# Value sums of the sample attention: two requests in the two column halves of the array, in clumps

## The chip, the cores and the metric

The kernel runs on one core of one Trainium2 chip. The metric is the device time of one execution in microseconds (us), as the median of several executions. The engines are named as in the profile: PE (TensorE, the matmul array), PEld (its weight loads), DVE (VectorE), ACT (ScalarE), POOL (GpSimd), and SP (the engine that issues nearly all transfers).

## The reference

One inference step of a decoder with two layers, for one prompt of 1024 tokens and eight sample requests of eight new tokens each, which share the weights. Each layer is a token mixer and then a SwiGLU channel mixer. The even layer's mixer is a causal convolution next to a stick-breaking attention with 8 heads of 64. For the sample requests, keys and values of 1024 past tokens lie in pages of 128 tokens; a table names the eight pages of each request. Cut to what the change touches:

```python
def stick_breaking_attention(q, k, v, bias, q_pos, k_pos):
    z = einsum('nqhd,nkhd->nhqk', q, k) * scale + bias
    mask = k_pos[None, :] < q_pos[:, None]
    log_1m = where(mask, log_sigmoid(-z), 0.0)
    after = cumsum(log_1m, axis=3, reverse=True) - log_1m
    wgt = exp(where(mask, log_sigmoid(z) + after, -inf))
    return einsum('nhqk,nkhd->nqhd', wgt, v)     # the value sums
...
gather = lambda cache, i: cache[i][page_table].reshape(8, 1024, 8, 64)
k_all = concatenate([gather(cache_k, i), k_new], axis=1)
v_all = concatenate([gather(cache_v, i), v_new], axis=1)
```

## The kernel before, in words

All tokens lie in two groups of columns: GA (the first 512 prompt tokens) and GB (the other 512 and the 64 sample tokens). A matmul of activations and weights is three array passes over split operands (`mm3`, L235). Work is in a foreground, the projections and channel mixers of a group, and a background, a chain of Python generators of which one piece is emitted at each slot of the foreground (`bg`, called as `slot` in `block`, `pair`, `out_block` and others). The order of the instructions on each engine is the order in which the Python code emits them; each engine works through its own in that order, and the framework adds the waits. While the foreground is the output projection and the channel mixer of GA, the background is `flow_c`: the prompt attention of GB, then `sample()` side by side with the convolution of GB (`conv_b`), then its normalization (`conv_norm`).

`sample()` works on four pairs of requests, `bp` 0 to 3; `b2` is the request within a pair. A score has 64 rows for a request (8 heads x 8 tokens), so a pair fills 128 rows. A unit is (pair, block of key pages, request); a unit has two steps `s`, 48 in all, 12 for a pair:

- `trans` turns three (or two) K pages by matmuls with the identity (L1112), ACT and DVE split them (`kth`, L1115 and L1116), `score` multiplies them with the queries (L1135), and `score_b` makes the sigmoids `bet` and `qf` of both requests of a pair.
- After the last unit of a pair, `weights` and `weights_b` make the stick-breaking weights by scans on DVE in three later steps, and `turned` turns them, keys onto partitions, into `wts` (L1184 on PE, L1185 on ACT): nine tiles of 128 keys x 128 columns, of which 64 belong to each request; the ninth is for the new keys.
- `pv(i)` multiplies one V page (128 keys x 512, all heads) with the 64 columns of its request (L1205), and sums in the PSUM tile `o` of 64 partitions. The pages go request after request: eight pages of `b2` 0, the new keys (`vnew`, L1211), then the copy out (`ob`, L1213), then the same for `b2` 1. Each `pv` is an item of `pvq`, and one item is taken at each of two places of a step. The tile `vst` holds two pages of one request, in two buffers; `load_v` issues two page loads on SP for it as soon as a buffer's two pages have been used.
- `o` holds every head's queries against every head's values. `fin`, one piece later, keeps the blocks where they agree: four matmuls of `ob` with columns of the constant `sel` (L1219), which turn the sums at the same time, and two ACT copies into `qall` (L1223). `sel` is made at the start of the kernel by two DVE copies of the identity.

From step 48 on there are no units left; a step then takes its items and gives way once.

## Time and profile before

| what | value |
|---|---|
| median of 3 executions | 2611.68 us (2611.19 to 2613.68) |
| span of the profiled execution | 2615.5 us |
| PE busy | 2524.0 us, 97% of the span |
| DVE, POOL, ACT busy | 65%, 60%, 42% |
| value matmuls from first to last | 675.9 to 968.5 us |
| moved over the span | 258.30 MB, 99 GB/s |

The profiled execution's own time is its span, 3.8 us above the median. A row of a group of instructions gives the line of the code, the engine, what is written from what, the count, the busy time and the mean duration in ns, and then the idle time of the engine just before these instructions with what ended it. Rows in order of time give start and length in us; consecutive alike instructions are one row. PE's durations overlap, since a matmul starts before the one ahead of it has drained; what one costs is read from start to start. "128*64" after the names is the part of the array in use, rows by columns, then come the shapes.

### The profile page before, as it was taken

The page shows a single profiled execution, that of the slowest core. Times are in us where ns is not written, and L with a number is a line of the kernel's source. Part 1 is how long each engine was busy: PE and PEld are TensorE (multiplying, and loading weights), DVE is VectorE, ACT ScalarE, POOL GpSimd, SP SyncE. Part 2 cuts the span into 40 slices and gives each one's busy share as a digit, 9 for nine tenths or more (in the row PEclk, how much of TensorE's full clock was granted, in tenths as well). Part 3 has the DMA queues.
Part 4 walks back from the last instruction along what each step waited for, and adds up shares of the span by engine and source line. Part 5 has one row for each costly group of instructions (what it writes and reads, how often), then busy time and mean ns, then how long its engine had stood idle before and what let it go on. Part 6 is the DMA issues. An engine that isn't in the chain of part 4 may idle for free.

```text
span 2615.5 us, 41225 instructions
## 1 busy us (share of the span) xinstructions
PE 2524.0 (97%) x15759; PEld 2223.2 (85%) x15759; DVE 1703.0 (65%) x2361; ACT 1109.9 (42%) x1885; POOL 1562.4 (60%) x1204
## 2 busy tenths in 40 slices
PE   8999999999999999999999999999999999999998
PEld 6788877887666657999999989989888888999997
DVE  4696777868767636276666643447777778667665
ACT  5536766744433324334433421233433334443333
POOL 6754244443333327578877732256888886987775
PEclk9999999999999999999999999999999999999999
DMA  7332241234455433422322321152233333333332
GB/s 216 113 110 72 63 115 37 73 104 128 140 145 151 131 106 100 130 73 81 91 88 83 113 78 41 45 144 63 88 96 97 93 93 92 98 92 111 89 89 77
DMA packets 355484, 258.30 MB, mean 99 GB/s; under 512 B 22913, under 2 KB 303617, under 8 KB 355272
## 3 DMA queue, kind: packets, MB, share of 16 engines
q1 hardware_dynamic: 355256, 255.66, 33.1%
q8 instruction: 125, 2.05, 0.3%
q14 instruction: 71, 0.58, 0.1%
q10 hardware_dynamic: 32, 0.01, 0.0%
HBM read 237.41 MB, written 18.69 MB: 98 GB/s over the span
## 4 chain that ended last, share of the span: by engine, by line
PE 41%; DVE 10%; POOL 2%; issue 1%; ACT 1%; POOLq 0%; DVEq 0%; ACTq 0%
PE acc L235 21%; PE acc L521 19%; DVE sum L200 2%; POOL hl L197 1%; DVE hid L241 1%; DVE hb L295 1%; DVE sum L201 1%; DVE sum L202 0%; DVE tmp L525 0%; DVE sum_c L214 0%; DVE b L1662 0%; POOL tmp L500 0%; DVE x L1662 0%; DVE fb L1666 0%; DVE xs L1666 0%
## 5 line engine op out<-in xcount | busy, mean ns | idle before, releaser
L186 POOL TENSOR_TENSOR hl<-stage,hl 128x512 fp32r<-128x512 f32 x464 | 636.4, 1395 | 507.8 <-ACT hl L184 382.4
L235 PE MATMUL acc<-x,hl 128*128 128x512 f32 (+1 forms) x3648 | 783.7, 351 | 12.2 <-DVE tmp L291 3.0
L235 PEld LDWEIGHTS acc<-x,hl 128*128 128x128 f32 x3648 | 580.3, 189 | 96.3 <-issue 30.4
L235 PE MATMUL acc<-hid,hl 128*128 128x288 f32 (+1 forms) x3096 | 555.9, 335 | 16.4 <-DVE hb L295 6.7
L235 PEld LDWEIGHTS acc<-hid,hl 128*128 128x128 f32 x3096 | 470.1, 190 | 84.1 <-issue 15.1
L295 DVE TENSOR_TENSOR hb<-acc,hb 128x512 f32<-128x512 f32 (+1 forms) x360 | 257.0, 719 | 194.8 <-PE acc L235 193.5
L521 PE MATMUL acc<-x,hl 128*128 128x288 f32 (+1 forms) x2676 | 362.1, 290 | 4.7 <-POOL hl L197 2.3
L521 PEld LDWEIGHTS acc<-x,hl 128*128 128x128 f32 x2676 | 348.9, 188 | 7.0 <-POOL hl L197 3.1
L197 POOL TENSOR_TENSOR hl<-sum,hl 128x512 fp32r<-128x512 f32 x180 | 237.1, 1345 | 176.1 <-ACT hl L196 176.1
L184 ACT ACTIVATE hl<-stage 128x1024 fp32r<-128x1024 f32 x232 | 243.5, 1054 | 229.6 <-PE acc L235 138.1
L525 DVE TENSOR_TENSOR tmp<-acc,tmp 128x288 f32<-128x288 f32 (+1 forms) x420 | 173.7, 442 | 230.7 <-ACT tmp L537 135.9
L197 POOL TENSOR_TENSOR hl<-stage,hl 128x512 fp32r<-128x512 f32 x180 | 267.7, 1509 | 13.3 <-ACT hl L196 13.3
L521 PE MATMUL acc<-b,hl 128*128 128x256 f32 (+1 forms) x1548 | 216.6, 291 | 14.8 <-DVE tmp L525 12.1
L521 PEld LDWEIGHTS acc<-b,hl 128*128 128x128 f32 x1548 | 202.2, 189 | 20.3 <-ACT hl L196 13.8
L235 PE MATMUL acc<-x1t,hl 128*128 128x288 f32 x1152 | 217.1, 296 | 1.5 <-POOL hl L186 1.5
L235 PEld LDWEIGHTS acc<-x1t,hl 128*128 128x128 f32 x1152 | 197.0, 189 | 19.7 <-POOL hl L186 1.7
L196 ACT ACTIVATE hl<-sum 128x512 fp32r<-128x512 f32 x180 | 103.1, 623 | 241.9 <-DVE sum L202 221.8
L291 DVE TENSOR_TENSOR tmp<-acc,rr 128x512 f32<-128x512 f32 (+1 forms) x108 | 75.1, 709 | 119.6 <-PE acc L235 109.5
L196 ACT ACTIVATE hl<-stage 128x512 fp32r<-128x512 f32 x180 | 105.6, 618 | 68.0 <-PE acc L235 62.7
L500 POOL TENSOR_TENSOR tmp<-tmp 128x576 f32<-128x576 f32 (+1 forms) x85 | 125.2, 1473 | 9.3 <-ACT tmp L477 8.3
L235 PE MATMUL acc<-x1a,hl 128*128 128x512 f32 x480 | 122.4, 408 | 3.0 <-POOL hl L186 1.3
L241 DVE TENSOR_TENSOR hid<-tmp,hid 128x512 fp32r<-128x512 f32 (+1 forms) x88 | 100.6, 1145 | 36.6 <-ACT hid L240 36.5
(288 smaller groups left out, 3298.1 us busy)
## 6 DMA issues: line engine op xcount, KB each, us to landing
stage<-in_w_ffn_in_dram SPq DMA_DIRECT2D x176, 512.0 KB
stage<-in_w_ffn_out_dram SPq DMA_DIRECT2D x88, 512.0 KB
stage<-in_w_in_even_dram SPq DMA_DIRECT2D x40, 512.0 KB
kst<-in_cache_k_dram SPq DMA_DIRECT2D x64, 256.0 KB
vst<-in_cache_v_dram SPq DMA_DIRECT2D x64, 256.0 KB
stage<-in_w_out_even_dram SPq DMA_DIRECT2D x16, 512.0 KB
stage<-in_w_in_odd_dram SPq DMA_DIRECT2D x16, 512.0 KB
stage<-in_w_out_odd_dram SPq DMA_DIRECT2D x16, 512.0 KB
```

Of the source, the lines that this page charges most:

```text
L184: act.activation(hl[:, 0], st, AF.Copy)
L186: pool.tensor_tensor(hl[:, 1, c], st[:, c], f32(hl[:, 0, c]), op=OP.subtract)
L196: act.activation(hl[:, 0, c], x, AF.Copy)
L197: pool.tensor_tensor(hl[:, 1, c], x, f32(hl[:, 0, c]), op=OP.subtract)
L200: todo = [lambda: dve.tensor_tensor(sb, su[:, lo], su[:, hi], op=OP.add), lambda: dve.tensor_tensor(sa[:, hi], sg[:, lo], su[:, lo], op=OP ...
L235: pe.matmul(acc[:, b, :c1 - c0], w, xs[:, xi, c0 - o:c1 - o], start=first and s == 0, stop=last and s == 2)
L241: (on or dve).tensor_tensor(dst[:, 1], src, f32(dst[:, 0]), op=OP.subtract)
L291: dve.tensor_tensor(d, a, r, op=OP.mult)
L295: dve.tensor_tensor(d, a, d, op=OP.add)
L500: (dve if both and f == NF - 1 else pool).tensor_tensor(t[:, :n], t[:, :n], u[:, :n], op=OP.mult)
L521: pe.matmul(acc[:, :w2], h[:, wi, i, k], xk[:, xi], start=k == 0 and s == 0, stop=k == 3 and s == 2)
L525: dve.tensor_tensor(out, acc[:, :w2], x, op=OP.add)
```

## The change

The two requests of a pair are summed together. `pv(i)` now takes the V page with the same number of both requests and puts their sums into the two halves of one PSUM tile `o` of 128 partitions, which are the two column halves of the array; `vst` accordingly holds one page of each. An item of `pvq` is now two such `pv` (four matmuls; with the new keys six), and during the units an item is taken only at the end of every second step. The second half of `turned`'s transposes goes through a list of its own, `soon`. The sums of both requests are copied out at once, and one selection serves both: `sel` becomes a matrix of 128 x (4 x 2 x 16) that is zero outside each request's own rows, made inside `sample()` by a memset on POOL and two ACT copies. From `pv` on there are four copies out and four selections in place of eight.

```diff
-    sel = consts.tile([128, 64], F, name="sel")
-        dve.tensor_copy(sel[0:64], ident[0:64, 0:64])
-        dve.tensor_copy(sel[64:128], ident[64:128, 64:128])
...
+            sel = sa.tile([128, 4, 2, 16], F, name="sel")
+            pool.memset(sel, 0.0)
+            for i in range(2):
+                r = slice(64 * i, 64 * i + 64)
+                act.activation(sel[r, :, i], ident[r, r].rearrange("p (h x) -> p h x", h=4), AF.Copy)
...
+                    bp, k = divmod(i, 8)
                     vst[i] = sa.tile([128, 2, 512], F, name="vst", bufs=2)
-                    for k in range(2):
-                        page_to(vst[i][:, k], cache_v, 2 * i + k)
+                    for b2 in range(2):
+                        page_to(vst[i][:, b2], cache_v, (2 * bp + b2) * 8 + k)
...
-                pvs = [lambda i=i: pv(i) for i in range(16 * bp, 16 * bp + 16)]
-                pvs[1] = lambda f=pvs[1]: (f(), new())
-                pvq.extend(first + pvs)
+                pvs = [lambda i=i: (pv(i), pv(i + 1)) for i in range(8 * bp, 8 * bp + 8, 2)]
+                pvs[0] = lambda f=pvs[0]: (f(), new())
+                soon.extend(first)
+                pvq.extend(pvs)
...
-                    osum[bp] = op_.tile([64, 512], F, name="o")
+                    osum[bp] = op_.tile([128, 512], F, name="o")
                 o = osum[bp]
-                load_v(i // 2 + 1)
-                pe.matmul(o, wts[bp][:, k, 64 * b2:64 * b2 + 64], vst[i // 2][:, k % 2], start=k == 0, stop=False)
-                if k % 2:
-                    vst.pop(i // 2)
-                    load_v(i // 2 + 3)
+                load_v(i + 1)
+                for b2 in range(2):
+                    r = slice(64 * b2, 64 * b2 + 64)
+                    pe.matmul(o[r], wts[bp][:, k, r], vst[i][:, b2], start=k == 0, stop=False)
+                vst.pop(i)
+                load_v(i + 3)
                 if k < 7:
                     return
-                pe.matmul(o, wts[bp][:, 8, 64 * b2:64 * b2 + 64], vnew, start=False, stop=True)
-                ob = tmp()[:64, 0:512]
+                for b2 in range(2):
+                    r = slice(64 * b2, 64 * b2 + 64)
+                    pe.matmul(o[r], wts[bp][:, 8, r], vnew, start=False, stop=True)
+                ob = tmp()[:, 0:512]
                 act.activation(ob, o, AF.Copy)
                 def fin():
                     for hp in range(4):
-                        pe.matmul(m[:, hp * 16:hp * 16 + 16], ob[:, hp * 128:hp * 128 + 128],
-                                  sel[:64, hp * 16:hp * 16 + 16], start=True, stop=True)
+                        pe.matmul(m[:, hp * 32:hp * 32 + 32], ob[:, hp * 128:hp * 128 + 128],
+                                  sel[:, hp].rearrange("p b x -> p (b x)"), start=True, stop=True)
...
-                if pvq:
-                    pvq.pop(0)()
+                while soon:
+                    soon.pop(0)()
                 if s < len(steps):
                     yield 2
...
-                if pvq:
+                if pvq and (s % 2 == 0 or s >= len(steps)):
                     pvq.pop(0)()
```

How the edit moves instructions on PE, first where the sums of the first pair begin (`z` are scores, `kst` K pages being turned, `acc` the foreground's matmuls, `wx` the weights of the new keys). Before, about 676 us:

```order
L1135 MATMUL z<-kth,qb 128x384 x4
L1205 MATMUL o<-vst,wts 64x512
L235 MATMUL acc<-hid,hl 128x512 x6
L1112 MATMUL m<-ident,kst 128x128 x3
L235 MATMUL acc<-hid,hl 128x512 x6
L1112 MATMUL m<-ident,kst 128x128 x3
L1205 MATMUL o<-vst,wts 64x512
L1184 MATMUL m<-ident,wx 128x128
L235 MATMUL acc<-hid,hl 128x512 x6
L1135 MATMUL z<-kth,qb 128x384 x4
L1205 MATMUL o<-vst,wts 64x512
```

The same place now, where the numbers of later lines have grown by two to eleven:

```order
L1138 MATMUL z<-kth,qb 128x384 x4
L235 MATMUL acc<-hid,hl 128x512 x6
L1115 MATMUL m<-ident,kst 128x128 x3
L235 MATMUL acc<-hid,hl 128x512 x6
L1115 MATMUL m<-ident,kst 128x128 x3
L235 MATMUL acc<-hid,hl 128x512 x6
L1138 MATMUL z<-kth,qb 128x384 x4
L1210 MATMUL o<-vst,wts 64x512 x4
L1187 MATMUL m<-ident,wx 128x128
```

Single value matmuls, two in a step, have become groups of four behind the scores of every second step. The second place is the last pair, on PE as well. Before, about 956 to 972 us:

```order
L1219 MATMUL m<-sel,tmp 128x16 x4
L1205 MATMUL o<-vst,wts 64x512 x2
L235 MATMUL acc<-x_6_77,hl 128x512 x3
L235 MATMUL acc<-x_7_78,hl 128x512 x3
L1205 MATMUL o<-vst,wts 64x512 x2
L235 MATMUL acc<-x_0_71,hl 128x512 x3
L235 MATMUL acc<-x_1_72,hl 128x512 x3
L1205 MATMUL o<-vst,wts 64x512 x2
L235 MATMUL acc<-x_2_73,hl 128x512 x3
L235 MATMUL acc<-x_3_74,hl 128x512 x3
L1205 MATMUL o<-vst,wts 64x512
L1211 MATMUL o<-vnew,wts 64x512
```

Now the whole of the last pair, from the turning of its weights to the selection:

```order
L1187 MATMUL m<-ident,bet 128x128 x8
L1210 MATMUL o<-vst,wts 64x512 x4
L1187 MATMUL m<-ident,wx 128x128
L235 MATMUL acc<-hid,hl 128x512 x6
L1210 MATMUL o<-vst,wts 64x512 x4
L235 MATMUL acc<-hid,hl 128x512 x6
L1210 MATMUL o<-vst,wts 64x512 x4
L235 MATMUL acc<-x_0_71,hl 128x512 x3
L235 MATMUL acc<-x_1_72,hl 128x512 x3
L1210 MATMUL o<-vst,wts 64x512 x4
L1217 MATMUL o<-vnew,wts 64x512 x2
```

Between two groups of four there are six matmuls of the foreground, as there were between two groups of two, and each group now reads four pages of V where one of before read two.

## The prediction, made before the changed kernel was run

> **What bounds the kernel now.** I read the page's busy time first, then the busy time by stretches around the sample attention, then the groups of the tensor engine there, and at last its order of time.

> ```profile
> span 2615.5 us, 41225 instructions
> PE 2524.0 (97%) x15759; PEld 2223.2 (85%) x15759; DVE 1703.0 (65%) x2361; ACT 1109.9 (42%) x1885; POOL 1562.4 (60%) x1204
> ```

> The tensor engine (PE) is busy for 97% of the span. Whether that holds where the edit lies is read from four stretches, one for each pair of requests whose value sums run there:

> ```profile
> core 0: us, PE busy (x) PEld busy (x) DVE busy (x) ACT busy (x) POOL busy (x), PEclk, DMA share, GB/s
> 675.90:743.20 67.30, 66.58 (x270) 41.37 (x269) 46.45 (x75) 22.25 (x46) 22.27 (x18) 1.00 0.51 146
> 768.20:834.60 66.40, 66.40 (x271) 41.49 (x270) 45.28 (x75) 23.22 (x48) 22.67 (x19) 1.00 0.50 148
> 857.40:924.60 67.20, 66.88 (x272) 41.65 (x271) 46.05 (x75) 22.06 (x45) 22.95 (x19) 1.00 0.42 126
> 934.50:971.60 37.10, 36.41 (x108) 16.54 (x108) 3.75 (x6) 6.33 (x12) 8.15 (x7) 0.92 0.43 128
> ```

> PE stands still for under 1 us in each; the next engine, DVE, is at 69% in the first three. So a microsecond taken from PE here is, to first order, a microsecond of the end. The groups that the edit touches, from 640 to 975 us:

> ```profile
> L1205 PE MATMUL o<-vst,wts 128*64 128x512 f32 x128 | 69.0, 627 | 1.9 <-ACT wts L1185 1.3 <-ACT tmp L1213 0.7
> L1219 PE MATMUL m<-sel,tmp 64*128 64x16 f32 x64 | 8.5, 262 | 0.0
> L1211 PE MATMUL o<-vnew,wts 128*64 128x512 f32 x16 | 8.2, 592 | 0.0
> L1184 PE MATMUL m<-ident,bet 128*128 128x128 f32 x32 | 4.7, 274 | 1.6 <-DVE bet L1170 1.6
> ```

> The 72 value matmuls are 144 instructions: a float32 matmul goes through the array as two passes. "128*64" is the part of the array in use: one column half. These durations overlap their neighbours, so the real price must be read from start to start:

> ```profile
> 941.04 1.07 PE L1205 MATMUL o<-vst,wts 128*64 128x512 f32 x2
> 942.04 1.67 PE L235 MATMUL acc<-hid,hl 128*128 128x512 f32 x6
> 943.64 1.93 PE L1205 MATMUL o<-vst,wts 128*64 128x512 f32 x4
> 945.50 1.67 PE L235 MATMUL acc<-x,hl 128*128 128x512 f32 x6
> 947.10 1.93 PE L1205 MATMUL o<-vst,wts 128*64 128x512 f32 x4
> ...
> 953.17 1.07 PE L1205 MATMUL o<-vst,wts 128*64 128x512 f32 x2 [0.68 <-ACT tmp L1213]
> ...
> 970.61 1.06 PE L1219 MATMUL m<-sel,tmp 64*128 64x16 f32 x8
> 971.60 1.67 PE L235 MATMUL acc<-x,hl 128*128 128x512 f32 x6
> ```

> ```profile
> 1005.80 15.70 PE L235 MATMUL acc<-x,hl 128*128 128x512 f32 x66
> 1021.34 2.98 PE L235 MATMUL acc<-hid,hl 128*128 128x512 f32 x12
> 1026.06 4.25 PE L235 MATMUL acc<-hid,hl 128*128 128x512 f32 x17 [1.75 <-DVE tmp L291]
> ```

> Two passes take 1.00 us (941.04 to 942.04), four take 1.86 (943.64 to 945.50): a further pass costs 0.43, and coming into the half array 1.00 - 0.86 = 0.14. Undisturbed L235 matmuls take (1021.34 - 1005.80) / 66 = 0.2355 each, six of them 1.41; the six after a visit take 1.60 (942.04 to 943.64). So each visit to the half array costs 0.14 + 0.19 = 0.33 beyond its passes.

> **The change, part by part.**

> *Fewer visits.* In the order of before the 72 value matmuls stand in 58 visits; in the order of after in 16 (twelve of four matmuls, four of six). 42 x 0.33 = 13.9 us.

> *Two halves at once.* The matmul count stays 72. A visit now runs, in order, A1 A2 B1 B2 A1 A2 B1 B2 (A and B the halves, 1 and 2 the two passes). Matmuls keep their order, so if halves overlap, A2 goes with B1, B2 with the next A1: five slots in place of eight, seven in place of twelve with the new keys. A pair of requests takes 3 x 5 + 7 = 22 slots in place of 36, all four 88 in place of 144: 56 x 0.43 = 24.1 us. The trace of before has no two parts of the array at work at once, so this term is bounded: zero if they take turns, 24.1 if they overlap; below zero, if changing halves empties the array as a visit does: 14 changes within the visits of a pair, 56 in all, at 0.33 is -18.5. I take 24.1, by the nearest row: L235 streams 512 four-byte columns in 0.2355 us, a value pass streams as many bytes in 0.43, so the path feeding the array already carries nearly twice what one pass draws.

> [...]

> *One selection for both.* L1219 goes from 8 groups of eight passes to 4. One group takes 0.99 (970.61 to 971.60), and its operand of 64 rows is also a change of the array's shape: with 0.19 for the neighbours 1.18, eight are 9.4 us. The new ones use 128 rows, no change of shape, and are nearest to the transposes of L1184 (eight passes in 1.09, below): 1.0 x 4 = 4.0. Gain 5.4. The wait of 0.68 at 953.17 (the second request's sum waits until the first is copied out) goes too: 0.7.

> *Building the selection* moves from DVE to one POOL memset and two ACT copies ahead of the first query fill. The nearest rows:

> ```profile
> L1086 ACT ACTIVATE qb<-hb x8: 239/252/258, 571.1 to 835.3; 64x64 fp32r<-64x64 f32 x8
> L1074 POOL MEMSET qb<- x1: 1060/1060/1060, 570.0 to 570.0; 128x1152 f32 x1
> ```

> That is 2 x 0.25 on ACT and about 1.06 x 128 / 1152 = 0.1 on POOL, once, beside a PE that has its own projection to do for six slots: nothing; without that cover 0.6. ACT also copies out 4 sums in place of 8: it is under 40% busy, nothing.

> *Loads in bursts.* A visit frees both V buffers, and four loads (two for each) stand behind it on the SP queue. Their pace:

> ```profile
> 944.74 1.44 SPq L597 DMA_DIRECT2D vst<-in_cache_v_dram  x2
> 946.29 0.39 SPq L166 DMA_DIRECT2D stage<-in_w_ffn_out_dram  x1
> 948.20 1.45 SPq L597 DMA_DIRECT2D vst<-in_cache_v_dram  x2
> ```

> ```profile
> L597 SPq DMA_DIRECT2D vst<-in_cache_v_dram x64: 337/338/669, 575.1 to 962.4; - x64
> PEld o L1205 <- DMA vst<-in_cache_v_dram: 0.9, 3, 0.3
> ```

> Two issues take 1.44 and one 0.34, so they come 1.1 us apart. The load issued at 944.74 is read by the second half of the visit at 947.10, without a longer wait than 0.3: it lands within about 3.3 us. At the 126 to 148 GB/s of the stretches a page of 128 x 512 x 4 bytes alone takes 1.8 to 2.1; I take 3, near the upper end, since the next pages share the way. For the first three pairs a visit comes every second step, 16 us apart, and four loads are there after 3 x 1.1 + 3 = 6.3: hidden. For the last pair the steps have no scores left, and the visits are one chunk of six L235 apart. From the landing of the last load: 0.86 for its passes, 1.1 + 3 to the landing of its successor: a round of 5.0 us. PE's own work in a round is 5 x 0.43 + 0.33 + 1.41 = 3.9. [...]

> *The last pair's weights.* These rows are the chain ahead of its first value matmul:

> ```profile
> 924.62 5.89 PE L235 MATMUL acc<-hid,hl 128*128 128x512 f32 x24
> 932.14 1.09 PE L1184 MATMUL m<-ident,bet 128*128 128x128 f32 x8 [1.63 <-DVE bet L1170]
> 934.50 1.97 PE L1205 MATMUL o<-vst,wts 128*64 128x512 f32 x2 [1.27 <-ACT wts L1185]
> ```

> It is DVE's chain, which the edit doesn't shorten; the selection that filled 0.99 of PE's time there moves ahead of it, so 1.0 of the gain turns into a longer wait.

> *DVE next.* It is densest here:

> ```profile
> 692.06:718.20 26.14, 25.42 (x103) 15.57 (x102) 21.73 (x34) 8.94 (x20) 7.08 (x5) 1.00 0.47 137
> 792.30:824.60 32.30, 32.30 (x132) 20.02 (x131) 28.04 (x48) 9.94 (x23) 9.26 (x8) 1.00 0.50 150
> 890.00:924.60 34.60, 34.28 (x141) 21.33 (x140) 24.98 (x42) 10.89 (x24) 12.70 (x11) 1.00 0.43 127
> ```

> The first three pairs lose about (44.1 - 10) / 3 = 11.4 of 67 us on PE, 17%. The stretches become 21.7, 26.8 and 28.7 against DVE's 21.7, 28.0 and 25.0. In the second DVE is over by 1.2, in the first it has no slack. Its queue may lag a little without PE waiting. I charge 3 us, between 0 and the whole saving of those two stretches, 10.

> *Sum.* 24.1 + 13.9 + 5.4 + 0.7 = 44.1, less 4.1 + 1.0 + 3.0 = 8.1: 36 us. The profiled execution spans 2615.5 and would become 2579.5; it lies 3.8 over the median of 2611.7, and against that the time is 2576.

> **The rivals.**

> *The halves take turns.* Then 24.1 is gone, the visits are long enough (3.8 + 1.41 = 5.2 a round) that the loads cost only about 1, DVE 1, the chain 1: 44.1 - 24.1 - 3 = 17, time 2595. For it: no row shows two halves at once. Against it: the feed argument above.

> *A weight load waits for the other half.* Each slot would show a load of a value pass:

> ```profile
> L1205 PEld LDWEIGHTS o<-vst,wts x128: 132/136/232, 675.9 to 967.2; 128*64 128x64 f32 x128
> ```

> 88 x 0.136 = 12 us less: 2588. Against it: within one half a pass follows after 0.43 and shows none of the 0.136. [...]

> *Changing halves empties the array*, 56 x 0.33: 44.1 - 24.1 - 18.5 - 2 = nothing: 2612, the edit does nothing.

> *Slower: V arrives late in every visit.* SP is one queue, and the four loads of a burst stand among K pages and weights. 36 us over 16 visits is 2.3 each. It decides if a burst landed 13 + 2.3 = 15 us after its visit rather than 6.3. Against it: V loads made PE wait 0.9 us in all. A time of 2625 would come of it.

> **How the numbers follow.** Overlap 0.62 (2576, own range 2566 to 2585: no losses and the 1.75 at 1026 gone, to all of DVE's 10 and more), weight loads shown 0.08 (2588), turns 0.16 (2595), emptying 0.06 (2612), late V 0.08 (2625). The range from 2565 to 2599 holds the first three, less some mis-sizing: about 8 in 10. Faster by over 0.2% (5 us, about what can be told from no change here) has 0.86, same 0.06, slower 0.08.

> **What would show it.** Right: value passes of the two halves that start together, a visit of four matmuls from start to start near 2.3 us (3.6 if they take turns, 4.6 if each change empties the array); six L235 in 1.60 only 16 times; L1224 as 128*128; waits for V of 1 to 2 us a visit for the last pair alone, PE's waits for DVE up by about 3. Wrong: bursts that wait before 930 us, or a DVE at 9 tenths for long with PE idle behind it.

## The result and the profile after

| | before | after |
|---|---|---|
| median | 2612.68 us (2611.19 to 2616.38, 4 runs) | 2576.41 us (2575.1 to 2576.9, 4 runs) |
| ratio, 95% interval | | 0.9855 [0.9841, 0.9869] |
| span of the profiled execution | 2615.5 us | 2574.2 us |
| value matmuls from first to last | 675.9 to 968.5 us | 679.4 to 924.4 us |

The forecast was 2576 us. The median fell by 36.3; the two profiled executions lie 41.3 apart, since the one of before was above its median and the one of after below. An execution's time is some 1.8 us longer than its span (2575.97 and 2574.2 in the profiled execution of after), so the one of before lies nearly 5 us above its median, not 3.8. The working below goes by the stage alone. Its ends are two rows that both traces have: the scores ahead of the first value matmuls, and the first of the foreground's matmuls with 288 columns, behind the same wait. First before, then after:

```profile
663.14 0.87 PE L1135 MATMUL z<-kth,qb 128*128 128x384 f32 x4
...
1048.19 12.11 PE L235 MATMUL acc<-x,hl 128*128 128x288 f32 x89 [1.47 <-DVE hb L295]
```

```profile
661.05 0.86 PE L1138 MATMUL z<-kth,qb 128*128 128x384 f32 x4
...
1009.37 50.90 PE L235 MATMUL acc<-x,hl 128*128 128x288 f32 x380 [1.47 <-DVE hb L295]
```

After is ahead by 2.1 us at the first row, where nothing of the change has run yet but its constant, and by 38.8 at the second. **The stage gains 36.7 us.**

One visit of after in order of time, then its value passes in two short windows (count, durations, first and last start):

```profile
692.82 1.94 PE L1210 MATMUL o<-vst,wts 128*64 128x512 f32 x8
694.69 1.66 PE L235 MATMUL acc<-x,hl 128*128 128x512 f32 x6
696.19 0.38 PE L1115 MATMUL m<-ident,kst 128*128 128x128 f32 x2
```

```profile
L1210 PE MATMUL o<-vst,wts x2: 643/643/643, 692.8 to 692.8; 128*64 128x512 f32 x2
...
L1210 PE MATMUL o<-vst,wts x4: 592/592/593, 693.3 to 693.7; 128*64 128x512 f32 x4
```

Eight passes take 1.87 us (692.82 to 694.69), as long as four took before. They start two by two: two at 692.8, two at 693.3, and so on. Four slots, where the prediction had five (2.3 us). The selection is one group of 0.81 (725.91 to 726.72) with no change of shape:

```profile
725.91 0.97 PE L1224 MATMUL m<-sel,tmp 128*128 128x32 f32 x8
726.72 0.52 PE L1115 MATMUL m<-ident,kst 128*128 128x128 f32 x3
```

Whether PE then stands still is read from its busy time over stretches that hold the same foreground matmuls: the first three pairs, then the last with what follows. Before, and after:

```profile
663.80:924.60 260.80, 258.09 (x1119) 172.99 (x1117) 183.12 (x297) 99.56 (x206) 90.77 (x71) 1.00 0.48 140
924.60:1048.20 123.60, 116.36 (x453) 79.33 (x452) 61.85 (x82) 44.55 (x67) 64.69 (x46) 0.97 0.35 106
```

```profile
661.80:892.30 230.50, 222.01 (x1095) 166.26 (x1094) 176.75 (x296) 95.55 (x198) 90.59 (x70) 0.99 0.55 159
892.30:1009.40 117.10, 109.43 (x445) 76.79 (x443) 60.44 (x83) 43.79 (x64) 65.06 (x47) 0.99 0.38 111
```

In the first three pairs PE idles 2.7 us before (260.80 - 258.09) and 8.5 after. Its waits there, longest sum first, before and then after:

```profile
PE m L1112 <- ACT hb L1223: 2.5, 3, 1.4
PE m L1112 <- DVE kth L1116: 0.2, 1, 0.2
```

```profile
PE z L1138 <- DVE zs L1149: 3.5, 3, 2.1
PE m L1115 <- DVE kth L1119: 2.3, 3, 1.5
PE acc L235 <- DVE hb L295: 1.9, 2, 1.8
PE acc L235 <- DVE tmp L291: 0.5, 1, 0.5
```

Three K transposes had waited for the selection's copy by ACT (2.5 us); that is gone. Waiting for DVE went from 0.2 to 8.2. DVE is busy for 77% of the stretch (176.75 of 230.50); it is late in places, not the bound throughout.

The last pair of after in order of time:

```profile
900.68 1.09 PE L1187 MATMUL m<-ident,bet 128*128 128x128 f32 x8 [2.65 <-DVE bet L1173]
903.04 3.49 PE L1210 MATMUL o<-vst,wts 128*64 128x512 f32 x8 [1.27 <-ACT wts L1188]
906.46 0.33 PE L1187 MATMUL m<-ident,wx 128*128 128x128 f32 x1
...
908.13 4.38 PE L1210 MATMUL o<-vst,wts 128*64 128x512 f32 x8
912.44 1.67 PE L235 MATMUL acc<-hid,hl 128*128 128x512 f32 x6
914.04 1.43 PE L1210 MATMUL o<-vst,wts 128*64 128x512 f32 x4
915.68 2.21 PE L1210 MATMUL o<-vst,wts 128*64 128x512 f32 x4 [0.21 <-DMA vst<-in_cache_v_dram]
917.82 1.67 PE L235 MATMUL acc<-x,hl 128*128 128x512 f32 x6
919.42 1.22 PE L1210 MATMUL o<-vst,wts 128*64 128x512 f32 x4
921.02 1.07 PE L1210 MATMUL o<-vst,wts 128*64 128x512 f32 x2 [0.38 <-DMA vst<-in_cache_v_dram]
923.07 0.64 PE L1210 MATMUL o<-vst,wts 128*64 128x512 f32 x1 [0.98 <-DMA vst<-in_cache_v_dram]
923.07 0.64 PE L1217 MATMUL o<-vnew,wts 128*64 128x512 f32 x1
...
924.93 1.66 PE L235 MATMUL acc<-x,hl 128*128 128x512 f32 x6
```

The first visit here takes 3.42 us (903.04 to 906.46); the granted clock was half from 902.8 to 906.2. The next three take 4.31, 3.78 and 5.51 (with the new keys), 13.60 in all, and the rows name V. Only part of it stands as idle time: a late page also stretches the row of passes (4.38 us at 908.13, where 1.94 is the row of 692.82). The two rows at 923.07 show two halves at once, once more: a pass of the new keys starts with the last page's pass in the other half.

For an account of the stage I gave each PE matmul the time to the start of the next, less idle time, and summed by kind over these stretches:

| us of PE's time | first three pairs, before | after | last pair and what follows, before | after |
|---|---|---|---|---|
| value passes | 53.3 | 26.4 | 18.5 | 15.3 |
| selection | 6.0 | 2.4 | 2.0 | 0.8 |
| K transposes and scores | 41.8 | 37.5 | - | - |
| foreground (L235) | 153.7 | 152.2 | 91.5 | 89.0 |
| other | 3.4 | 3.4 | 4.4 | 4.3 |
| idle | 2.7 | 8.5 | 7.2 | 7.7 |
| sum | 260.8 | 230.5 | 123.6 | 117.1 |

The table goes from foreground matmul to foreground matmul (663.85, 924.62 and 1048.19; 661.75, 892.25 and 1009.37). So 30.3 us come from the first three pairs and 6.4 from the last, where the value passes, which should have halved, fell by 3.2 alone.

### The profile page after: what moved, and what is told of

Its sections match the earlier page's. It is cut to its first block, busy times and chain, and to the rows that moved or that the text cites. A ratio compares the mean times of both kernels' runs of the same rounds, so it can differ in the third digit from the quotient of the medians.

```text
span 2574.2 us, 41142 instructions
## 1 busy us (share of the span) xinstructions
PE 2477.7 (96%) x15727; PEld 2213.7 (86%) x15727; DVE 1693.0 (66%) x2359; ACT 1105.3 (43%) x1875; POOL 1564.2 (61%) x1205
## 4 chain that ended last, share of the span: by engine, by line
PE 44%; DVE 8%; POOL 2%; issue 1%; ACT 1%; POOLq 0%; DVEq 0%; ACTq 0%
PE acc L235 23%; PE acc L521 20%; POOL hl L197 1%; DVE sum L200 1%; DVE hid L241 1%; DVE hb L295 1%; DVE sum L201 1%; DVE b L1669 0%; DVE tmp L525 0%; DVE sum L202 0%; DVE x L1669 0%; DVE sum_c L214 0%; DVE fb L1673 0%; DVE xs L1673 0%; POOL tmp L500 0%
## 5 line engine op out<-in xcount | busy, mean ns | idle before, releaser
L235 PE MATMUL acc<-x,hl 128*128 128x512 f32 (+1 forms) x3648 | 780.6, 350 | 12.2 <-DVE hb L295 2.6
L235 PEld LDWEIGHTS acc<-x,hl 128*128 128x128 f32 x3648 | 581.4, 189 | 77.2 <-issue 10.9
L235 PE MATMUL acc<-hid,hl 128*128 128x288 f32 (+1 forms) x3096 | 552.3, 334 | 16.8 <-DVE hb L295 6.9
L235 PEld LDWEIGHTS acc<-hid,hl 128*128 128x128 f32 x3096 | 470.4, 190 | 69.9 <-DVE hb L295 11.0
L235 PE MATMUL acc<-x1t,hl 128*128 128x288 f32 x1152 | 216.4, 296 | 1.5 <-POOL hl L186 1.5
L235 PEld LDWEIGHTS acc<-x1t,hl 128*128 128x128 f32 x1152 | 196.0, 188 | 19.4 <-POOL hl L186 1.7
L291 DVE TENSOR_TENSOR tmp<-acc,rr 128x512 f32<-128x512 f32 (+1 forms) x108 | 75.0, 709 | 113.2 <-PE acc L235 100.0
L500 POOL TENSOR_TENSOR tmp<-tmp 128x576 f32<-128x576 f32 (+1 forms) x85 | 127.8, 1504 | 11.7 <-ACT tmp L477 8.3
L235 PE MATMUL acc<-x1a,hl 128*128 128x512 f32 x480 | 121.7, 407 | 2.5 <-POOL hl L186 1.3
```

What stands on the lines that cost most here:

```text
L235: pe.matmul(acc[:, b, :c1 - c0], w, xs[:, xi, c0 - o:c1 - o], start=first and s == 0, stop=last and s == 2)
L291: dve.tensor_tensor(d, a, r, op=OP.mult)
L500: (dve if both and f == NF - 1 else pool).tensor_tensor(t[:, :n], t[:, :n], u[:, :n], op=OP.mult)
```

## The experiments

Theory: the halves work side by side (two passes a slot), fewer visits and one selection add to it; V pages that come late in the last pair, and DVE, take part of it back. Rivals: the fewer visits make most of the gain; the passes pair up only because of the order in which they are written; DVE's wait is nothing that the change brought.

**The change again**, beside three of the kernels that follow (halves without clumps, order of the passes, V ahead).

> The changed kernel once more, on the chip and beside the runs that the next three kernels are compared with. Every theory expects what was measured, a ratio to before of 0.9855 within 0.002, and a visit of four value matmuls of 1.87 us from start to start.

2575.43 us (2575.02 to 2579.14), ratio 0.9865 [0.9849, 0.988]. Its profile has the same visits of 1.87; its stage, between the same two rows, gains 38.9. So a stage can differ by 2 us between executions of one kernel. Two differences show in the traces: where the clock halved (below), and how late V came in the last pair, where the same three visits take 3.44, 3.92 and 4.74 us, 12.10 in all.

**The halves without the clumps.** An item is one page of both requests, at every step; as many value matmuls, 32 visits in place of 16.

```diff
-                pvs = [lambda i=i: (pv(i), pv(i + 1)) for i in range(8 * bp, 8 * bp + 8, 2)]
+                pvs = [lambda i=i: pv(i) for i in range(8 * bp, 8 * bp + 8)]
...
-                if pvq and (s % 2 == 0 or s >= len(steps)):
+                if pvq:
```

> The halves without the clumps: one page number per item (two matmuls, four passes), an item at the end of every step; 32 visits in place of 16. Theory (matmuls of the two halves start together, so four passes take the time of two, and a visit costs 0.33 us beside its passes): a visit of two matmuls takes 0.86 + 0.14 = 1.00 us from start to start; PE has 16 x 0.33 = 5.3 us more to do, but the V loads come two by two, so the waits for V in the last pair (some 4 us) shrink, and DVE's work meets shorter gaps: 2574 to 2582. Rival (the overlap needs a clump, within one page number the halves take turns): a visit of 1.86, 16 x 0.86 + 5.3 = 19 us more than the change: 2595.

2574.58 us (2572.3 to 2575.68), ratio 0.9854 [0.9839, 0.9869]: the same time as with clumps. A visit, in order of time:

```profile
695.82 1.08 PE L1210 MATMUL o<-vst,wts 128*64 128x512 f32 x4
696.83 0.97 PE L235 MATMUL acc<-x,hl 128*128 128x512 f32 x3
```

Two matmuls take 1.01: two slots and the 0.14 of coming in. The halves overlap without a clump. The 16 visits more would be 5.3 us at 0.33, 4.0 of them in the first three pairs. There PE is busy for 225.1 us, with the change in its two executions for 222.0 and 220.4, so the price of a visit is seen; but PE idles 7.1 instead of 8.5 and 8.5. In the last pair and what follows the kernel takes 115.6 and the change 117.1 and 116.6: PE and its weight loads wait 1.8 us for V in all, with the change 10.0 and 8.5. So what the clumps save is given back in waits for DVE and V, and the total time shows nothing of it.

**The clumps without the halves.** This and the last three kernels below ran beside other executions of before (median 2613.36 us) than the other four (2611.72). The edit is made to before, with items of four V pages of one request at every second step.

```diff
-                pvs = [lambda i=i: pv(i) for i in range(16 * bp, 16 * bp + 16)]
-                pvs[1] = lambda f=pvs[1]: (f(), new())
-                pvq.extend(first + pvs)
+                pvs = [lambda i=i: [pv(j) for j in range(i, i + 4)] for i in range(16 * bp, 16 * bp + 16, 4)]
+                pvs[0] = lambda f=pvs[0]: (f(), new())
+                soon.extend(first)
+                pvq.extend(pvs)
...
-                if pvq:
+                if pvq and (s % 2 == 0 or s >= len(steps)):
```

> The clumps without the halves: the kernel before, request after request in one half, but four value matmuls of one request as an item at the end of every second step; 16 visits in place of 58, the old selection. Theory (the gain is the sum of 13.9 us for fewer visits and some 31 for the overlap): a visit of four matmuls takes 8 x 0.43 + 0.14 = 3.58 us; PE wins 42 x 0.33 = 13.9, less 2 to 4 for bursts: 2598 to 2602. Rival (the visits are most of what was gained, the overlap little): below 2590.

2596.04 us (2594.44 to 2599.83), ratio 0.9936 [0.9923, 0.9948]. A visit of four pages and the new keys:

```profile
697.51 3.65 PE L1206 MATMUL o<-vst,wts 128*64 128x512 f32 x8
701.00 1.02 PE L1212 MATMUL o<-vnew,wts 128*64 128x512 f32 x2
701.95 1.67 PE L235 MATMUL acc<-x,hl 128*128 128x512 f32 x6
```

Eight passes in one half, with two more of the new keys behind them, take 3.49 us. A visit without new keys shows the whole:

```profile
713.74 3.65 PE L1206 MATMUL o<-vst,wts 128*64 128x512 f32 x8
717.31 1.67 PE L235 MATMUL acc<-x,hl 128*128 128x512 f32 x6
```

It takes 3.57, against 1.87 in two halves. By the account of before, value passes of the first three pairs fall from 53.3 to 48.1 and their neighbours (foreground, K transposes, scores) by 6.5: 11.7 us for 36 visits fewer, 0.325 each, where the prediction had 0.33. From here to the change, which adds the halves, the value passes fall by another 23.0, to 25.1 in its second execution, where no visit of these pairs ran at half clock: 54 slots of 0.43 (18 a pair) would be 23.2. With the clumps alone PE idles only 0.6 in these pairs, so a PE that is faster by 14 us meets no late DVE yet.

The whole gain is 17.3 us, above the 13.9 of the theory and the time below its 2598: the K transposes' wait of 2.5 for ACT's copies went as well, and in the last pair the clock stayed full (no value pass took over 0.64 us, where before has 1.12), where before ran 6.83 us at 0.50 (from 933.5).

**The order of the passes.** Both pages of one request, then both of the other: A A A A B B B B for A1 A2 B1 B2 A1 A2 B1 B2.

```diff
...
-                for b2 in range(2):
-                    r = slice(64 * b2, 64 * b2 + 64)
-                    pe.matmul(o[r], wts[bp][:, k, r], vst[i][:, b2], start=k == 0, stop=False)
-                vst.pop(i)
-                load_v(i + 3)
+                for b2 in range(2):
+                    r = slice(64 * b2, 64 * b2 + 64)
+                    for j in range(2):
+                        pe.matmul(o[r], wts[bp][:, k + j, r], vst[i + j][:, b2], start=k + j == 0, stop=False)
+                for j in range(2):
+                    vst.pop(i + j)
+                load_v(i + 4)
...
```

> Within a clump both pages of the first half, then both of the second: the passes stand A A A A B B B B in the program. Theory 1 (each half takes its passes from a queue of its own, the second half's are not held up by those that stand ahead of them): a visit stays at 1.87 us, the time within 2 us of the change. Theory 2 (passes start in the order of the program, only neighbours overlap; as the prediction had it): B's first pass starts with A's fourth, 7 slots in place of 4, a visit of 3.15 us and 16 x 1.29 = 21 us slower than the change, about 2597.

2580.24 us (2577.37 to 2583.91), ratio 0.9881 [0.9866, 0.9897]. A visit, and its passes in its first 0.3 us:

```profile
694.18 1.94 PE L1211 MATMUL o<-vst,wts 128*64 128x512 f32 x8
696.05 0.72 PE L235 MATMUL acc<-x,hl 128*128 128x512 f32 x2
```

```profile
L1211 PE MATMUL o<-vst,wts x2: 643/643/643, 694.2 to 694.2; 128*64 128x512 f32 x2
```

Still 1.87, and still two passes that start together, though the second half's first pass now stands behind four of the first half. Had starts kept the order of the program, only the last A and the first B could have met, and the visit would have had seven slots, 3.15 us. The records do not name the half; that the two are of different halves follows from one half's passes being 0.43 apart. The 5 us more than the change, where theory 1 had at most 2, are for the most part V's: the last pair and what follows takes 120.8 us for 117.1 and 116.6, since a clump now needs both pages of each request sooner and frees all four later; the waits of PE and its weight loads for V go from 8.5 to 16.0 us. There one also sees the passes standing in the written order: at 910.79 the two passes of the first half's first page run alone, 1.07 us, and the second half starts only at 913.63, together with the first half's second page, for which PE had waited 1.77 us. Its own page had been asked for 1.2 us before that one (909.28, 910.49).

**V pages ahead.** The last pair's V pages are fetched ahead into buffers that K pages no longer need (`kst`).

```diff
-                    vst[i] = sa.tile([128, 2, 512], F, name="vst", bufs=2)
+                    if i in (26, 27, 28, 31):
+                        vst[i] = [sa.tile([128, 512], F, name="kst", bufs=KP) for _ in range(2)]
+                    else:
+                        t = sa.tile([128, 2, 512], F, name="vst", bufs=2)
+                        vst[i] = [t[:, 0], t[:, 1]]
...
-                load_v(i + 3)
+                load_v(i + 3 if i < 24 else i + 6)
...
+                if s == len(steps) - 1:
+                    load_v(29)
```

> Eight V pages of the last pair are put into the K page buffers, six of them loaded right after the last scores: V is there ahead of each visit. Theory (the short steps of the last pair make PE wait for V, some 4.5 us of the gain): the waits for V go, 4 to 5 us faster than the change, about 2572. Rival (PE waits there for the foreground's own chain, V is only the last to come): within 1 us of the change, with waits on other engines in the same place.

2567.35 us (2565.38 to 2570.0), ratio 0.983 [0.9817, 0.9844]: 8 us faster than the change beside it, where 4 to 5 were expected, and the fastest version that does the whole work, together with the last one below. The same three visits of the last pair:

```profile
907.95 1.94 PE L1214 MATMUL o<-kst,wts 128*64 128x512 f32 x8
909.82 1.67 PE L235 MATMUL acc<-hid,hl 128*128 128x512 f32 x6
911.42 1.08 PE L1214 MATMUL o<-kst,wts 128*64 128x512 f32 x4
...
913.28 1.67 PE L235 MATMUL acc<-x,hl 128*128 128x512 f32 x6
914.88 1.08 PE L1214 MATMUL o<-vst,wts 128*64 128x512 f32 x4
...
917.61 1.67 PE L235 MATMUL acc<-x,hl 128*128 128x512 f32 x6
```

They take 1.87, 1.86 and 2.73, 6.46 in all instead of 13.60: late V had cost 7.1 us, and 5.6 in the second execution. The first three pairs are as in the change (230.5 us).

**Half of the convolution's DVE work**, in both kernels. `conv_b` leaves out its odd taps, 60 DVE instructions; the convolution's sums then lack these taps.

```diff
             for j in range(CW):
-                tap(acc, ext[:, j:j + HALF], j)
                 if j % 2 == 0:
+                    tap(acc, ext[:, j:j + HALF], j)
                     continue
```

> The changed kernel with every second tap of the convolution of GB left out (60 DVE instructions of 0.75 us, so the convolution's sums lack these taps); nothing else. Theory (in the changed kernel DVE holds PE back in the densest steps and in the chain to the last pair's weights, with its cold clock some 8 to 11 us in all): 2565 to 2569. Rival (the idle PE there waits for orders of work that DVE's load doesn't set): within 2 us of the change.

> The same taps left out of the kernel before. Theory: there PE was late enough for DVE, only the chain to the last pair's weights (1.6 us and some of its cold clock) wins: 2606 to 2610. Rival (fewer taps shorten either kernel alike, DVE is no price of the change): as much faster as the changed kernel gets by it.

After with half the taps: 2566.29 us (2562.6 to 2567.46), ratio 0.9815 [0.9802, 0.9828]. Before with half the taps: 2604.5 (2601.44 to 2609.31), ratio 0.9969 [0.9959, 0.9979]. By the ratios after gains 0.40% to 0.50% (0.9855 and 0.9865 to 0.9815), 10 to 13 us, and before 0.31%, 8 us, more than the theory had for it. With intervals of some 0.15% to either side the totals leave the question open. The stretches tell more. In both, some 4.6 us are won ahead of the value sums, between 600 and 661 us (foreground matmul against foreground matmul). The first three pairs, of after and of before:

```profile
657.60:880.70 223.10, 219.48 (x1096) 165.98 (x1095) 152.10 (x254) 95.45 (x198) 92.08 (x69) 1.00 0.56 164
```

```profile
657.20:916.00 258.80, 257.36 (x1118) 173.12 (x1116) 153.67 (x255) 99.49 (x206) 90.87 (x70) 1.00 0.49 142
```

There after goes from 230.5 to 223.1, its idle time from 8.5 to 3.6; before goes from 260.8 to 258.8, from 2.7 to 1.4. DVE's lateness in these pairs is a price of the change: 7.4 less 2.0, about 5.4 us; against the second execution of after, without the half clock at 708.2, it is some 4. Before gains its other 3.5 in the last pair and what follows (123.6 to 120.1), where the wait for the weights got shorter (0.84 for 1.63) and the clock stayed full (1.00); after gains 1.0 there.

**V pages ahead and the convolution held** while DVE makes the last weights (the convolution's pieces are not emitted from the last unit until `turned`).

```diff
+                phase.pop("hold", None)
                 pvs = [lambda i=i: (pv(i), pv(i + 1)) for i in range(8 * bp, 8 * bp + 8, 2)]
...
+                    phase["hold"] = True
...
-                    if wait or not piece:
+                    if (wait or not piece) and "hold" not in phase:
```

> The version with the last pair's V ahead (e2), and besides the convolution gives no taps while the last pair's weights are made; they follow later, nothing is left out. Theory (DVE's chain of scans, stretched by four taps of 0.75 us, makes PE wait 2.65 us there and, idle long enough, go to half clock): 2 to 5 us faster than e2, 2562 to 2565. Rival (the chain is bound by its own scans and hand-overs): within 1 us of e2.

2567.29 us (2564.33 to 2571.97), ratio 0.9826 [0.9812, 0.9841]: not to be told from V ahead alone. The place itself did get shorter:

```profile
899.33 1.09 PE L1191 MATMUL m<-ident,bet 128*128 128x128 f32 x8 [1.06 <-DVE bet L1177]
901.69 1.94 PE L1215 MATMUL o<-vst,wts 128*64 128x512 f32 x8 [1.27 <-ACT wts L1192]
```

The wait is 1.06 for 2.65, and the first visit takes 1.87 for 3.42. The stretch from the first three pairs' end to the second anchor row takes 107.0 us for 110.0. By the ratios, 0.9826 for 0.983, some 1 us of these 3 is seen. Where the rest went stays open: the ranges of the times (some 5 and 8 us wide) are wider than that.

## Why the prediction was right, and where its terms were off

The time was as forecast, through terms that were off in both directions.

- **What bounds the stage: right.** PE was all but full, and 36.7 us of its time (38.9 in the second execution) became 36.3 of the median.
- **Fewer visits, 13.9: right.** The clumps alone measured 0.325 a visit. But what it gave was taken back by waits: with the halves and without clumps the time is the same.
- **Two halves at once, 24.1: too small.** The step that failed is "matmuls keep their order", which the rows of before, with one half at work, show, and from which five slots for a visit of four matmuls came and seven for one of six. The runs show four and six, in either order of the passes: 72 slots saved in place of 56, 72 x 0.43 = 31.0. That two halves work at once without loss is shown, since a slot still takes 0.43; that the feed of L235 is the reason is not. In the run with the other order two passes start together (694.2) though three others stand between them in the program. Eight passes went from 3.57 us to 1.87, 1.91 times, or 1.98 times without the 0.14 of coming in.
- **One selection, 5.4: nearly.** The groups fell from 0.99 to 0.81, not to 1.0 as taken, 7.9 to 3.2 us in all by the account, 4.7. The 0.19 a group for the neighbours does not show: foreground, K transposes and scores of the first three pairs fell by 5.7 us (6.0 in the second execution), no more than the 6.5 with the clumps alone, where the selection is the old one.
- **The wait of 0.7 went**, as said. So did two that were not in the sum: 2.5 us of K transposes waiting for the selection's copies, and the 1.75 at 1026, which the prediction had only in its range.
- **Building the selection at nothing: right.** The two copies took 0.26 us each on ACT, at 569 us, beside a busy PE.
- **Loads in bursts, 4.1: too small, 7.1, and 5.6 in the second execution.** The place was right: V is late in the last pair alone and in none of the first three. The three visits took 4.31, 3.78 and 5.51 for 1.87, 1.86 and 2.73, which is 2.4, 1.9 and 2.8 lost a round instead of 1.4 (1.6, 2.1 and 2.0 in the second execution). The landing, taken as 3, was nearly right: the last loads that a visit reads, issued at 908.53, 913.79 and 919.02, are read at 911.44, 916.82 and 923.07, after 2.9, 3.0 and 4.05 us; in the second execution after 3.0, 3.3 and 3.3. The 4.1 is three rounds that lose 5.0 - 3.9 = 1.1 each and 0.8 for SP, which was the author's estimate and which no run shows; the rows have 0.03 to 0.15 from the end of a buffer's last pass to the next issue. The term mis-sized is PE's own work in a round, which rests on the five slots: it was 1.87 + 1.60 = 3.5, not 3.9, so a round of 5.25 loses 1.8. In the last visit the new keys' passes stand behind the late page besides.
- **The last pair's weights, 1.0: right.** The wait went from 1.63 to 2.65.
- **DVE next, 3.0: too small.** The idle time of the first three pairs rose by 5.8, and half the taps gave back 4 to 5.4 more than they did in before. Waiting for DVE itself rose by 8.0; the 2.5 for ACT's copies went. The step that failed is to compare sums over stretches of 26 to 35 us: only one of them was over, by 1.2. The waits come singly, where an operation that PE needs stands behind the convolution's pieces in DVE's order. For the wait of 2.15 at 707.08, whose end is the last of these rows of DVE's:

```profile
702.10 1.53 DVE L865 SCALAR_TENSOR_TENSOR cacc<-ext,par,cacc 128x512 f32<-128x512 f32 x2
703.54 2.20 DVE L873 TENSOR_TENSOR tmp<-ext,par 128x248 f32<-128x248 f32 x2
705.78 0.67 DVE L874 TENSOR_REDUCE snew<-tmp 128x16 f32<-128x496 f32 x1
706.48 0.55 DVE L1149 TENSOR_TENSOR zs<-z,zs 64x384 f32<-64x384 f32 x1
```

Five pieces of the convolution, 4.4 us, come ahead of the copy of the scores.

The overlap was 6.9 larger and the waits outside the sum 4.2; the one selection was 0.7 smaller, V 3.0 worse and waiting for DVE 5.0. That the time came out within 1 us is in part these errors cancelling, and so in part luck. They would leave the stage 2.4 above the 36 of the prediction where 36.7 were measured, and 3.9 above it in the second execution, where 38.9 were. The 1.7 and 1.0 that are left over stay open. A visit at half clock, 1.3 us at 707.77, is in the first alone; in the last pair half clock cost after 1.6 (903.04), but before no less: 934.50 to 941.04 took 6.54 us there, and the same rows 3.86 in before with half the taps.

Of the rivals, "take turns" and "emptying" fall by the visit of 1.87; so does the weight load that waits, since four slots of 0.43 and the 0.14 leave no room for loads of 0.136. "Late V in every visit" falls by the waits, all behind 903 us.

## What to carry to other kernels

Eight value passes, which each fill half the columns of the array, took PE 1.87 us in two halves next to each other and 3.57 in one; long clumps were not needed for that, and their saving in visits was lost again where four pages were wanted at once. When PE's work in a stage shrinks, go to its last and shortest steps and ask what feeds each burst there: fetching those pages ahead was worth 8 us beside the 36 of the change itself. DVE, at 70% before, took 4 to 5.4 us back while its busy time in the first three pairs stayed below PE's (176.75 and 222.01), so price an engine's longest run of pieces ahead of what PE waits for, not its share.

## What the hardware showed that was not expected

The halves did not take their passes in the order of the program: in the run with the other order, with four passes of one half ahead, two passes still started together at 694.2, where passes of one half are 0.43 apart. A wait for data, in contrast, held both (as at 913.63 in the run with the other order): at 923.07 in after, behind a wait of 0.98, the new keys' pass started only with the page's pass ahead of it.

```profile
708.30:711.50 3.20, 3.20 (x9) 0.94 (x6) 2.84 (x6) 1.62 (x4) 1.51 (x2) 0.50 0.26 80
```

```profile
708.70:712.10 3.40, 3.40 (x16) 1.75 (x17) 1.84 (x4) 2.79 (x6) 0.51 (x1) 1.00 0.14 31
```

But for the one at the very end, the stretches at half clock of before and after last 3.41 us or, twice in before, 6.83, and the first four of after begin whole multiples of 3.41 apart (230.4, 622.9, 708.2, 902.8 us). In the 3.41 us ahead of 708.2 PE was busy for 1.26, ahead of 902.8 for 1.09. Divided into stretches of 3.41 us, counted from the first at half clock and without their first 6 and last 10 us, the two traces have 11 at full clock in which PE was busy for under 45%, and half clock followed on all of them; it followed on 2 of the 25 between 45% and 61%, and on none of the 1457 above. Behind 1.06 and 1.27, with transposes between, in the kernel with the convolution held, the clock was 1.00; behind 2.65 and 1.27 in after, and behind 1.63 and 1.27 in before, it was 0.50. In after the two visits that stood in such a stretch took 3.19 and 3.42 us for 1.87, 1.3 and 1.6 more.
